# Second layer of a two-layer attention trunk: a pair's value products moved to stand ahead of the next pair's turn

## The chip, the core and the metric

The kernel runs on one core of a Trainium2 chip. The metric is the device time of one execution in microseconds, and less is better. A core has a matrix engine (TensorE, PE in the profile; its weight loads are PEld), a vector engine (VectorE, DVE), a scalar engine (ScalarE, ACT), a general one (GpSimd, POOL) and a queue that starts transfers (SyncE, SP). Each works through its own instructions in order and waits for the others on semaphores.

## The reference

Two decoder layers over 256 tokens of width 2048, in fp32. Each layer is x + (mixer(rmsnorm(x)) * silu(gate)) @ w_out; the first mixer is latent attention with 16 heads, the second, which the change touches, is sliding-window attention with 32 query heads of width 64, 4 key and value heads and a learned sink per head. A last RMSNorm ends it.

```python
def swa_sink_attention(q, k, v, sinks):          # blocks of 128 queries against 256 keys
    s = jnp.einsum('bnqhgd,bnkhd->bnhgqk', qb, kw) * (D ** -0.5)
    s = jnp.where(valid, s, NEG_INF)             # causal, window of 128
    m = jnp.maximum(jnp.max(s, axis=-1, keepdims=True), sink)
    e = jnp.exp(s - m)
    p = e / (jnp.sum(e, axis=-1, keepdims=True) + jnp.exp(sink - m))
    return jnp.einsum('bnhgqk,bnkhd->bnqhgd', p, vw)

x = x + (y * jax.nn.silu(gate)) @ w_out
```

## The kernel before

**Precision and products.** The activations lie transposed: channels on the partitions, the 256 tokens along the free axis. An fp32 product is made of three matmuls on values split into a high and a low half (`proj`, lines 247 to 252: high weights by high data, high weights by low data, low weights by high data). All weights (some 114 MB with the rest of what is read) stream in pieces of 128 x 1024. `Weights` (lines 49 to 96) loads a piece through SP's queue (L70), splits it (high half by ScalarE, L89; low half by VectorE, L90) and hands the pieces out in the order in which they were added. It keeps four pairs of halves. A *slab* (line 254) is one piece's work: 8 chunks of the contraction by 3 matmuls, 24 matmuls of 128 x 256. Two slabs make one output chunk of 128 channels; their sums lie in one of three PSUM banks (tag `pp`).

**The second layer's attention.** It goes through 16 pairs of heads, c = 0 to 15. For a pair there are:

- `query(c)` (line 616): two slabs, then rotary embedding on VectorE (lines 293 to 296) and a split into a stack of high and low halves (`stack_pair`, lines 302 and 303). It is a generator that stops behind its first slab and again at its end.
- `gate(c)` (line 627): two slabs, and silu (lines 361 to 363), likewise a generator with a stop behind each slab.
- `scores(c)` (line 635): six matmuls (L642, L644, L645), then softmax: masked minimum on VectorE (L322, L324), exponentials on ScalarE (L328), the sum with the sink, a reciprocal, and the normalised probabilities (L333, L334).
- `turn(p)` (line 336): six transposes of the probabilities on TensorE (L342, L343), and their split into `pth` (ScalarE, L348) and `ptl` (VectorE, L349), one buffer each.
- `values(c)` (line 660): six matmuls of values by probabilities (L670, L672) into the one bank `yp`, two copies (ScalarE, L675) and two adds (VectorE, L679), which leave `y`.
- `gated(c)` (line 682): `y` times the gate (L684), and its split into the two halves `ys[c]` (ScalarE L194, VectorE L195), which the output projection reads.

The loop (line 692) works ahead: in turn c it does the query of pair c + 2 and the scores of pair c + 1. In program order a turn is: query slab, turn c, scores c + 1, query slab, gate slab, values c, gate slab, gating c. In the last two turns there is no query; gate slabs stand in its place, and the values follow on the second gate slab.

**The output projection.** 14 chunks (line 712) of two slabs each over `ys[0]` to `ys[15]`; the last pair's `ys[15]` is the last contraction chunk of the second slab. The last two chunks (lines 721 to 774) are done apart, with the final norm.

**What sets the order.** The program's order is a wish: at compile time a planner gives each engine its instructions, by program order, but moves later ones ahead where it expects an earlier one to wait. What was given to an engine it does in that order. In the second layer's attention TensorE's order is the program's, except at the start (pair 0) and at the end (pair 15), where transposes and values stand between the matmuls of a slab.

Of the kernel before, what the change touches and what calls it, by code (L numbers as in the profile page):

```python
# [28 lines left out]
KC = D // P  # L29
# [19 lines left out]
class Weights:  # L49
# [43 lines left out]
    def next(self):  # L93
        self.split(self.used + 1 + self.ahead_split)
        self.used += 1
        return self.ready.popleft()
# [3 lines left out]
def trunk(ctx: ExitStack, tc: tile.TileContext, a: dict):  # L100
# [49 lines left out]
    def xc(c):  # L150
        return x_t[c // XQ][:, c % XQ, :]
# [37 lines left out]
    def tiny(name, n=2, bufs=2):  # L189
        return work.tile([P, n], F32, tag=name, name=name, bufs=bufs)  # L190
# [56 lines left out]
    def proj(ps, lhs, rhs, first, last):  # L247

        wh, wl = lhs
        mm(ps, lhsT=wh, rhs=rhs[:, 0, :], start=first, stop=False)  # L250
        mm(ps, lhsT=wh, rhs=rhs[:, 1, :], start=False, stop=False)  # L251
        mm(ps, lhsT=wl, rhs=rhs[:, 0, :], start=False, stop=last)  # L252

    def slab(ps, half, src):

        hi, lo = w.next()
        k0 = half * (KC // 2)
        for k in range(k0, k0 + KC // 2):
            n = slice((k - k0) * P, (k - k0 + 1) * P)
            proj(ps[:, 0:S], (hi[:, n], lo[:, n]), src[k], k == 0, k == KC - 1)  # L260

    def bank(pool_, tag):
        return pool_.tile([P, 512], F32, tag=tag, name=tag)
# [26 lines left out]
    def rope(out, ps, cs, sn, mask):  # L290
        t1 = work.tile([P, S], F32, tag="ro1", name="ro1")
        t2 = work.tile([P, S], F32, tag="ro2", name="ro2")
        dve.tensor_tensor(out=t1, in0=ps, in1=cs, op=ALU.mult)
        dve.stream_shuffle(out=t2, in_=ps, mask=mask)
        dve.tensor_tensor(out=t2, in0=t2, in1=sn, op=ALU.mult)
        dve.tensor_tensor(out=out, in0=t1, in1=t2, op=ALU.add)  # L296

    def stack_pair(dst, src):

        for j, r in ((0, slice(0, 64)), (1, slice(64, 128))):  # L300
            o = slice(64, 128) if j == 0 else slice(0, 64)
            act.copy(out=dst[r, j, :], in_=src[r, :])  # L302
            dve.tensor_tensor(out=dst[o, j, :], in0=src[r, :], in1=dst[r, j, :].bitcast(F32), op=ALU.subtract)  # L303
# [9 lines left out]
    def softmax(ps, j, nm, sm, mask, scale, sink):  # L313

        p = work.tile([P, 3 * P], F32, tag="p", name="p", bufs=3)
        for i in range(2):
            cols = slice(0, P) if i == 0 else slice(P, 3 * P)
            src = ps[:, 0:P] if i == 0 else ps[:, S:2 * S]
            m = mask
            if i == 0:  # L320
                m = p[:, cols]
                dve.tensor_tensor(out=m, in0=ps[:, P:S], in1=mask[:, P:], op=ALU.add)  # L322
            c = 2 * i + j
            dve.tensor_tensor_reduce(out=p[:, cols], in0=src, in1=m,  # L324
                                     scale=scale if isinstance(scale, float) else scale[:, i:i + 1],
                                     scalar=BIG if sink is None else sink, op0=ALU.add, op1=ALU.min,
                                     accum_out=nm[:, c:c + 1])
            act.activation(out=p[:, cols], in_=p[:, cols], func=AF.Exp, scale=-1.0, bias=nm[:, c:c + 1],  # L328
                           accum_out=sm[:, c:c + 1])
        return p  # L330
# [25 lines left out]
    def silu(ps, rB):  # L356

        hx = work.tile([P, S], F32, tag="hx", name="hx", bufs=2)
        th = work.tile([P, S], F32, tag="th", name="th", bufs=1)
        out = work.tile([P, S], F32, tag="sg", name="sg", bufs=2)  # L360
        dve.scalar_tensor_tensor(out=hx, in0=ps, scalar=0.5, in1=rB, op0=ALU.mult, op1=ALU.mult)
        act.activation(out=th, in_=hx, func=AF.Tanh)
        dve.scalar_tensor_tensor(out=out, in0=th, scalar=1.0, in1=hx, op0=ALU.add, op1=ALU.mult)
        return out
# [251 lines left out]
    def query(c):  # L616
        ps = bank(ps_p, "pp")
        slab(ps, 0, hs)
        yield
        slab(ps, 1, hs)  # L620
        qf = work.tile([P, S], F32, tag="ro3", name="ro3")
        rope(qf, ps[:, 0:S], cos1R, sin1R, MASK_SWA)
        qs_of[c] = work.tile([P, 2, S], F32R, tag="qs", name="qs", bufs=2)
        stack_pair(qs_of[c], qf)
        yield

    def gate(c):
        ps = bank(ps_p, "pp")
        slab(ps, 0, hs)
        yield  # L630
        slab(ps, 1, hs)
        sg_of[c] = silu(ps[:, 0:S], r1B)
        yield

    def scores(c):
        kv = 2 * c // (QH // KVH)
        nm, sm, ri = tiny("nm", 4), tiny("sm", 4), tiny("ri", 4)
        pair = []
        for j in range(2):
            sc = bank(ps_s, "sc")  # L640
            o, t = sc[:, 0:S].rearrange("p (a q) -> p a q", a=2), slice(0, P)
            mm(o, lhsT=qs_of[c][:, j, t], rhs=k1s[kv][:, :, t], start=True, stop=True)  # L642
            o, t = sc[:, S:2 * S], slice(P, S)
            mm(o, lhsT=qs_of[c][:, j, t], rhs=k1s[kv][:, 0, :], start=True, stop=False)  # L644
            mm(o, lhsT=qs_of[c][:, j, t], rhs=k1s[kv][:, 1, :], start=False, stop=True)  # L645
            h = 2 * c + j
            pair.append(softmax(sc, j, nm, sm, mask_w, -SWA_SCALE, nsink[:, h:h + 1]))

        e = tiny("es", 4)
        dve.tensor_tensor(out=e.rearrange("p (i j) -> p i j", j=2), in0=nm.rearrange("p (i j) -> p i j", j=2),  # L650
                          in1=sinks[:, 2 * c:2 * c + 2].rearrange("p (i j) -> p i j", i=1).to_broadcast([P, 2, 2]),
                          op=ALU.add)
        act.activation(out=e, in_=e, func=AF.Exp)
        dve.tensor_tensor(out=e, in0=e, in1=sm, op=ALU.add)
        dve.reciprocal(out=ri, in_=e)
        for j in range(2):
            normalise(pair[j], ri, j)
        p_of[c] = pair

    def values(c):  # L660

        kv = 2 * c // (QH // KVH)
        v0, v1 = (v[:, kv, :, :].rearrange("p a d -> p (a d)") for v in vs)
        pt = pt_of.pop(c)
        yp = bank(ps_y, "yp")
        late = yp.rearrange("p (j i q) -> p j i q", j=2, i=2)[:, :, 1, :]
        for n, p in enumerate(pt):
            for j in range(2):
                o = slice(j * S, (j + 1) * S)
                mm(yp[:, o], lhsT=v0, rhs=p[:, o], start=n == 0 and j == 0, stop=False)  # L670
        for n, p in enumerate(pt):
            mm(late, lhsT=v1, rhs=p[:, 4 * P:].rearrange("p (j q) -> p j q", j=2), start=False, stop=n == 1)  # L672
        t = work.tile([P, S], F32, tag="vh", name="fo", bufs=1)
        for j in range(2):
            act.copy(out=t[j * HD:(j + 1) * HD, :], in_=yp[(1 - j) * HD:(2 - j) * HD, j * S:(j + 1) * S])  # L675
        y = work.tile([P, S], F32, tag=("vl", "v1")[c % 2], name="y", bufs=1)
        for j in range(2):
            n = slice(j * HD, (j + 1) * HD)
            dve.tensor_tensor(out=y[n, :], in0=yp[n, j * S:(j + 1) * S], in1=t[n, :], op=ALU.add)  # L679
        y_of[c] = y  # L680

    def gated(c):
        yg = work.tile([P, S], F32, tag="yg", name="yg", bufs=2)
        dve.tensor_tensor(out=yg, in0=y_of.pop(c), in1=sg_of.pop(c), op=ALU.mult)  # L684
        split(ys[c], yg)

    for c in range(2):
        for _ in query(c):
            pass
        if c == 0:  # L690
            scores(0)
    for c in range(KC):
        q, gt = query(c + 2) if c + 2 < KC else iter([None, None]), gate(c)
        next(q)
        if c + 2 >= KC:
            next(gt)
        pt_of[c] = turn(p_of.pop(c), True)
        if c + 1 < KC:
            scores(c + 1)
        next(q)  # L700
        if c + 2 < KC:
            next(gt)
        if c + 2 < KC:
            values(c)
        next(gt)
        if c + 2 >= KC:
            values(c)
        gated(c)


    sq_x2 = Squares("sq_x2")
    for c in range(KC - 2):
        ps = bank(ps_p, "pp")
        for half in range(2):
            slab(ps, half, ys)
        dve.tensor_tensor(out=xc(c), in0=ps[:, 0:S], in1=xc(c), op=ALU.add)
        sq_x2.add(xc(c))
        dve.tensor_scalar(out=xc(c), in0=xc(c), scalar1=gf[:, c:c + 1], scalar2=None, op0=ALU.mult)
# [137 lines left out]
```

## Time and profile before

| what | value |
|---|---|
| median of 3 runs | 684.73 us (680.62 to 688.16) |
| profiled execution | 684.75 us, its span 683.0 us |
| mean granted TensorE clock | 0.996 |
| layer 1, projection in (0 to 60 us) | TensorE busy 55.79 of 60.00 us |
| layer 1, attention (60 to 257) | 195.96 of 197.00 |
| layer 1, projection out (257 to 353.5) | 96.50 of 96.50 |
| layer 2, keys, values, first queries (353.5 to 390) | 36.27 of 36.50 |
| layer 2, the 16 pairs (390 to 590) | 199.54 of 200.00 |
| layer 2, projection out, norm, end (590 to 683) | 83.22 of 93.00 |

How to read the profile: times in us from the start of the span; a row of stages gives the stretch, its length, and for each engine the busy time and the count of instructions, then TensorE's granted clock, the share of the transfer engines and GB/s. A count holds the instructions that were begun before the stretch and still run in it; a matmul stands for some 0.28 us in the trace, though the next one starts after less than half of that, so two or so are counted too many. A row of instructions gives start, length, engine, line, operation, output <- inputs, and in brackets how long the engine idled before it and for whom. A row of a group gives count, busy time, mean length in ns, and the idle time ahead of the group.

### The profile page before, as it was taken

What the parts mean: (1) busy time and instruction counts of PE and PEld (TensorE: products, weight loads), DVE (VectorE), ACT (ScalarE), POOL (GpSimd) and SP (SyncE); (2) the same over time, 40 slices, a digit from 0 to 9 for tenths busy, and PEclk for the clock granted to TensorE, in tenths of its full rate; (3) what the DMA queues carried; (4) which work ended last, traced back from release to release, by engine and by line L of the source; (5) the groups of instructions that cost most, each with busy time, mean ns of one, the idle gap of its engine ahead of it and who ended that gap; (6) DMA issues with size and microseconds to landing.
All of it is one profiled execution on the core that took longest, in us unless ns stands there. A gap on an engine that the chain in (4) does not pass through costs nothing.

```text
span 683.0 us, 14550 instructions
## 1 busy us (share of the span) xinstructions
PE 667.3 (98%) x5718; PEld 663.1 (97%) x5718; DVE 532.2 (78%) x1085; ACT 428.0 (63%) x853; POOL 66.3 (10%) x72
## 2 busy tenths in 40 slices
PE   8999999999999999999999999999999999999994
PEld 7999999999999999999999999999999999999994
DVE  5897787787688686666658899998998998766664
ACT  6667656666676665444446688788778778544430
POOL 3634000000000000111110000000000000022220
PEclk9999999999999999999999999999999999999998
DMA  8664454554554555555554545545445454455604
GB/s 311 252 206 168 161 161 144 185 167 144 183 162 150 174 167 174 196 183 189 184 187 160 180 141 169 166 147 177 160 157 158 157 177 158 156 188 195 204 32 124
DMA packets 37302, 117.00 MB, mean 171 GB/s; under 512 B 4209, under 2 KB 8945, under 8 KB 37233
## 3 DMA queue, kind: packets, MB, share of 16 engines
q1 hardware_dynamic: 37232, 116.06, 51.3%
q8 instruction: 45, 0.74, 0.4%
q14 instruction: 25, 0.20, 0.1%
HBM read 113.95 MB, written 2.10 MB: 170 GB/s over the span
## 4 chain that ended last, share of the span: by engine, by line
PE 88%; DVE 4%; ACT 3%; POOL 1%; issue 1%; DMA 1%; SPq 0%; DVEq 0%; ACTq 0%; POOLq 0%
PE pp L251 24%; PE pp L250 24%; PE pp L252 24%; PE pt L342 1%; DVE wlo L90 1%; ACT whi L89 1%; PE pp L735 1%; PE pp L520 1%; PE pp L522 1%; PE pp L521 1%; PE yp L670 1%; PE pt L343 1%; DVE x L762 1%; DMA wraw<-in_w_c 1%; PE sc L642 1%
## 5 line engine op out<-in xcount | busy, mean ns | idle before, releaser
L90 DVE TENSOR_TENSOR wlo<-wraw,whi 128x1024 fp32r<-128x1024 f32 (+1 forms) x217 | 259.9, 1199 | 88.6 <-ACT whi L89 87.0
L89 ACT CAST whi<-wraw 128x1024 fp32r<-128x1024 f32 (+1 forms) x217 | 222.9, 1029 | 168.7 <-PE pp L251 142.1
L252 PE MATMUL pp<-hs,wlo 128*128 128x256 f32 x860 | 239.6, 279 | 1.3 <-DVE wlo L90 1.2
L250 PE MATMUL pp<-hs,whi 128*128 128x256 f32 x860 | 240.4, 280 | 0.4 <-ACT whi L89 0.4
L251 PE MATMUL pp<-hs,whi 128*128 128x256 f32 x860 | 239.6, 279 | 0.5 <-DVE hs L200 0.5
L252 PEld LDWEIGHTS pp<-hs,wlo 128*128 128x128 f32 x860 | 161.5, 188 | 1.9 <-DVE wlo L90 1.9
L250 PEld LDWEIGHTS pp<-hs,whi 128*128 128x128 f32 x860 | 162.6, 189 | 0.6 <-ACT whi L89 0.6
L251 PEld LDWEIGHTS pp<-hs,whi 128*128 128x128 f32 x860 | 161.6, 188 | 0.9 <-DVE hs L200 0.9
L251 PE MATMUL pp<-ys,whi 128*128 128x256 f32 x480 | 133.9, 279 | 0.1
L250 PE MATMUL pp<-ys,whi 128*128 128x256 f32 x480 | 133.9, 279 | 0.0
L252 PE MATMUL pp<-ys,wlo 128*128 128x256 f32 x480 | 133.8, 279 | 0.0
L216 POOL TENSOR_TENSOR sq_x<-sq_x,sq 128x256 f32<-128x256 f32 x43 | 53.3, 1240 | 577.2 <-ACT sq L215 335.5
L250 PEld LDWEIGHTS pp<-ys,whi 128*128 128x128 f32 x480 | 91.2, 190 | 0.0
L251 PEld LDWEIGHTS pp<-ys,whi 128*128 128x128 f32 x480 | 90.1, 188 | 0.3 <-DVE ys L195 0.3
L252 PEld LDWEIGHTS pp<-ys,wlo 128*128 128x128 f32 x480 | 90.1, 188 | 0.0
L328 ACT ACTIVATE p<-p,nm 128x128 f32<-128x128 f32 x96 | 42.7, 446 | 15.3 <-DVE nm L324 15.3
L250 PE MATMUL pp<-cq,whi 128*128 128x256 f32 x96 | 27.3, 284 | 0.0
L200 DVE SCALAR_TENSOR_TENSOR hs<-x,gains,hs 128x256 fp32r<-128x256 f32 x32 | 24.9, 790 | 2.6 <-ACT hs L199 2.6
L252 PE MATMUL pp<-cq,wlo 128*128 128x256 f32 x96 | 26.7, 278 | 0.0
L251 PE MATMUL pp<-cq,whi 128*128 128x256 f32 x96 | 26.7, 278 | 0.0
L303 DVE TENSOR_TENSOR qs<-ro,qs 64x256 fp32r<-64x256 f32 x48 | 20.2, 421 | 7.5 <-ACT qs L302 6.3
L302 ACT CAST qs<-ro 64x256 fp32r<-64x256 f32 x48 | 19.2, 400 | 8.3 <-DVE ro L296 7.7
(242 smaller groups left out, 1133.6 us busy)
## 6 DMA issues: line engine op xcount, KB each, us to landing
wraw<-in_w_g SPq DMA_DIRECT2D x64, 512.0 KB, 3.7
wraw<-in_w_o SPq DMA_DIRECT2D x64, 512.0 KB, 3.5
wraw<-in_w_q SPq DMA_DIRECT2D x32, 512.0 KB, 3.6
wraw<-in_w_ukv SPq DMA_DIRECT2D x16, 512.0 KB, 3.5
wraw<-in_w_c SPq DMA_DIRECT2D x15, 512.0 KB, 6.7
wraw<-in_w_uq SPq DMA_DIRECT2D x8, 512.0 KB, 3.6
wraw<-in_w_uq SPq DMA_DIRECT2D x8, 256.0 KB, 2.6
wraw<-in_w_k SPq DMA_DIRECT2D x4, 512.0 KB, 3.4
```

Source lines behind the costliest of these rows:

```text
L89: self.nc.scalar.copy(out=hi, in_=src)
L90: self.nc.vector.tensor_tensor(out=lo, in0=src, in1=hi.bitcast(F32), op=ALU.subtract)
L200: dve.scalar_tensor_tensor(out=dst[:, 1, :], in0=src, scalar=col, in1=dst[:, 0, :].bitcast(F32), op0=ALU.mult, op1=ALU.subtract)
L216: pool.tensor_tensor(out=self.acc, in0=self.acc, in1=t, op=ALU.add)
L250: mm(ps, lhsT=wh, rhs=rhs[:, 0, :], start=first, stop=False)
L251: mm(ps, lhsT=wh, rhs=rhs[:, 1, :], start=False, stop=False)
L252: mm(ps, lhsT=wl, rhs=rhs[:, 0, :], start=False, stop=last)
L302: act.copy(out=dst[r, j, :], in_=src[r, :])
L303: dve.tensor_tensor(out=dst[o, j, :], in0=src[r, :], in1=dst[r, j, :].bitcast(F32), op=ALU.subtract)
L328: act.activation(out=p[:, cols], in_=p[:, cols], func=AF.Exp, scale=-1.0, bias=nm[:, c:c + 1], accum_out=sm[:, c:c + 1])
L342: nc.tensor.transpose(t[:, 0, j * S + i * P:j * S + (i + 1) * P], p[:, i * P:(i + 1) * P], ident)
L343: nc.tensor.transpose(t[:, 1, j * P:(j + 1) * P], p[:, 2 * P:3 * P], ident)
```

## The change

In the loop over the pairs, the generators of the gates are made ahead, so that both slabs of a gate stand next to each other. The value products and the gating of pair c - 1 stand in turn c, behind the first query slab and directly ahead of the transposes. In turn 14 the first slab of gate 14 takes the place of the query slab; behind the scores stand its second slab and both slabs of gate 15. In turn 15 only values 14, gating 14 and the transposes are left. Values 15 and gating 15 stand between the two slabs of the first output chunk. The order in which the weights are used is the same, and so is every instruction.

```diff
-    for c in range(KC):
-        q, gt = query(c + 2) if c + 2 < KC else iter([None, None]), gate(c)
-        next(q)
-        if c + 2 >= KC:
-            next(gt)
+    ends = [gate(c) for c in range(KC)]
+    for c in range(KC):
+        if c + 2 < KC:
+            q = query(c + 2)
+            next(q)
+        elif c + 1 < KC:
+            next(ends[c])
+        if c > 0:
+            values(c - 1)
+            gated(c - 1)
         pt_of[c] = turn(p_of.pop(c), True)
         if c + 1 < KC:
             scores(c + 1)
-        next(q)
         if c + 2 < KC:
-            next(gt)
-        if c + 2 < KC:
-            values(c)
-        next(gt)
-        if c + 2 >= KC:
-            values(c)
-        gated(c)
+            next(q)
+            next(ends[c])
+            next(ends[c])
+        elif c + 1 < KC:
+            next(ends[c])
+            next(ends[c + 1])
+            next(ends[c + 1])
...
     for c in range(KC - 2):
         ps = bank(ps_p, "pp")
         for half in range(2):
             slab(ps, half, ys)
+            if c == 0 and half == 0:
+                values(KC - 1)
+                gated(KC - 1)
```

## The prediction

> **What bounds the kernel now.** I read the page first, then a table of stages, then the waits of the second layer's attention, and last the start times of single matmuls. The page says that TensorE is the bound; the column 1.00 of the stages below, that its clock is granted in full.
>
> ```profile
> span 683.0 us, 14550 instructions
> PE 667.3 (98%) x5718; PEld 663.1 (97%) x5718; DVE 532.2 (78%) x1085; ACT 428.0 (63%) x853; POOL 66.3 (10%) x72
> ```
>
> The profiled execution took 684.75 us, its span 683.0 and 1.75 around it; the median of the runs shown is 684.73, so a sum against the one stands against the other. The three runs lie 7.5 us apart, so within 1% (6.85 us) is about what a measurement can't tell from no change.
>
> The stages, with busy time (and count) of TensorE, its weight loads, VectorE, ScalarE and GpSimd:
>
> ```profile
> 400.09:570.77 170.68, 170.68 (x1484) 170.68 (x1483) 157.89 (x404) 133.51 (x312) 0.00 (x0) 1.00 0.49 163
> 401.43:406.87 5.44, 5.44 (x50) 5.44 (x49) 5.41 (x19) 3.42 (x11) 0.00 (x0) 1.00 0.56 197
> 407.56:413.21 5.65, 5.65 (x50) 5.65 (x49) 4.84 (x12) 4.93 (x11) 0.00 (x0) 1.00 0.52 186
> 558.99:564.43 5.44, 5.44 (x50) 5.44 (x49) 5.44 (x18) 3.47 (x10) 0.00 (x0) 1.00 0.57 188
> 565.12:570.77 5.65, 5.65 (x50) 5.65 (x49) 4.79 (x10) 4.83 (x11) 0.00 (x0) 1.00 0.53 186
> 570.77:589.28 18.51, 18.05 (x152) 17.42 (x151) 15.66 (x36) 12.99 (x29) 0.00 (x0) 1.00 0.44 143
> 100.63:106.09 5.46, 5.46 (x51) 5.46 (x49) 3.87 (x15) 4.10 (x14) 0.00 (x0) 1.00 0.60 197
> 106.86:112.20 5.34, 5.34 (x49) 5.34 (x48) 3.80 (x5) 2.58 (x5) 0.00 (x0) 1.00 0.45 164
> 260.00:350.00 90.00, 90.00 (x767) 90.00 (x765) 58.97 (x65) 45.12 (x64) 15.36 (x15) 1.00 0.56 186
> 595.00:655.00 60.00, 60.00 (x532) 60.00 (x531) 40.00 (x45) 26.86 (x34) 16.03 (x11) 1.00 0.56 185
> ```
>
> The first row covers 13 pairs, from turn 1 to turn 14: 13.13 us each, TensorE without a gap, VectorE 92% busy. So in the steady part there is no stall that a new order could remove.
>
> But the next four rows show something else. Each holds two slabs, 48 matmuls of one shape (the count has some 2 more, begun before the window). Between the scores and the values they take 5.44 us, 113.3 ns each; between the values and the next turn 5.65 us, 117.7 ns each. The difference, 0.21 us, stands in the first pair shown as in the last. It does not belong to a slab, an engine's load or the clock (1.00 in all): the first layer's output projection holds the slow spacing over 90 us (90.00 / 765 = 117.6 ns), the second layer's the fast one over 60 us (60.00 / 530 = 113.2). It is a rhythm that TensorE keeps until something between two slabs tips it.
>
> The start times show where it tips:
>
> ```profile
> 406.76 0.28 PE L252 MATMUL pp<-hs,wlo 128*128 128x256 f32 x1
> 406.87 0.39 PE L670 MATMUL yp<-pth,vs 128*128 128x256 f32 x2
> ...
> 407.44 0.28 PE L672 MATMUL yp<-ptl,vs 128*128 128x256 f32 x1
> 407.56 0.28 PE L250 MATMUL pp<-hs,whi 128*128 128x256 f32 x1
> 413.21 0.38 PE L342 MATMUL pt<-ident,p 128*128 128x128 f32 x2
> ...
> 413.76 0.27 PE L343 MATMUL pt<-ident,p 128*128 128x128 f32 x1
> 413.79 0.37 PE L642 MATMUL sc<-k1s,qs 128*128 128x256 f32 x1
> ```
>
> The values (L670, L672) take 0.69 us at the fast spacing; the slab behind them runs slow. The transposes (L342, L343) and scores follow on the slow stretch; the slabs behind those run fast. The first layer has the other entry: its 48 matmuls ahead of a turn run fast (row 100.63) and so do those behind it (row 106.86), with no scores between. So a turn is left fast from either side.
>
> **The change part by part.** No instruction is added or removed, and the weights are used in the same order (for pair 14 and 15 too), so SP's queue of loads stays as it is. Three things move.
>
> *Pairs 0 to 13.* The values of pair c leave the middle of gate c, and stand behind the first query slab of the next turn, directly ahead of the transposes. Now the values still end fast, but transposes and scores come right behind, and then four slabs in a row. By the rows above these are all fast. There are 14 slow stretches now, behind the values of pairs 0 to 13: 14 x (5.65 - 5.44) = 2.94 us saved; the slab behind the values of pair 14 is slow too (24 x 4.4 ns = 0.1). The sum takes 3.05. From both sides: 0 if the turn needs a slow entry to be left fast, and the fast stretches lost as well if the tip carries through the turn (14 x -0.21 = -2.94).
>
> *What else the values move.* On VectorE and ScalarE the two copies, two adds, the gating and its split now come just ahead of the probabilities' split and the softmax. What TensorE next needs from there, and when:
>
> ```profile
> 566.56 0.49 ACT L334 ACTIVATE p<-p,ri 128x256 f32<-128x256 f32 x1
> 567.38 0.87 DVE L303 TENSOR_TENSOR qs<-ro,qs 64x256 fp32r<-64x256 f32 x2 [0.46 <-ACT qs L302]
> 570.77 0.38 PE L342 MATMUL pt<-ident,p 128*128 128x128 f32 x2
> 571.35 0.37 PE L642 MATMUL sc<-k1s,qs 128*128 128x256 f32 x1
> ```
>
> The normalised probabilities are ready at 567.05, 3.7 us ahead of their turn; the query stack at 568.25, 3.1 us ahead of its scores. The moved work ahead of them is at most
>
> ```profile
> L90 DVE TENSOR_TENSOR wlo<-wraw,whi 128x1024 fp32r<-128x1024 f32 x53 | 64.6, 1219 | 1.5 <-ACT whi L89 0.2
> L349 DVE TENSOR_TENSOR ptl<-pt,pth 128x768 fp32r<-128x768 f32 x13 | 12.4, 950 | 0.0
> L679 DVE TENSOR_TENSOR y<-yp,fo 64x256 f32<-64x256 f32 x26 | 11.0, 422 | 4.4 <-ACT fo L675 4.2
> L684 DVE TENSOR_TENSOR yg<-y,sg 128x256 f32<-128x256 f32 x13 | 5.5, 425 | 0.4
> L675 ACT COPY fo<-yp 64x256 f32<-64x256 f32 x26 | 9.5, 366 | 0.5
> L348 ACT CAST pth<-pt 128x768 fp32r<-128x768 f32 x13 | 10.3, 795 | 0.0
> L303 DVE TENSOR_TENSOR qs<-ro,qs 64x256 fp32r<-64x256 f32 x26 | 10.9, 421 | 6.2 <-ACT qs L302 5.8
> ```
>
> two adds (0.84 us) and, if nothing fills it, the wait for two copies (0.73); the gating stood ahead of the softmax before as well. 1.6 us fits into 3.1. I cost it at nothing; without that cover it is up to 1.6 us a pair once the slack is used up. The probabilities' split (0.80 and 0.95 us) had two slabs to finish in and now has four slabs and more, but there was no stall to save there except in the last pair.
>
> *The end, pairs 14 and 15 and the first output chunk.* Here TensorE does wait:
>
> ```profile
> 578.48 0.28 PE L251 MATMUL pp<-hs,whi 128*128 128x256 f32 x1
> 578.91 0.33 PE L342 MATMUL pt<-ident,p 128*128 128x128 f32 x1 [0.15 <-ACT p L333]
> 580.16 0.27 PE L343 MATMUL pt<-ident,p 128*128 128x128 f32 x1
> 580.19 0.36 PE L251 MATMUL pp<-hs,whi 128*128 128x256 f32 x1
> 583.75 0.28 PE L252 MATMUL pp<-ys,wlo 128*128 128x256 f32 x1
> 584.20 0.50 PE L670 MATMUL yp<-ptl,vs 128*128 128x256 f32 x2 [0.17 <-DVE ptl L349]
> 588.53 0.28 PE L250 MATMUL pp<-ys,whi 128*128 128x256 f32 x1
> 588.94 0.38 PE L251 MATMUL pp<-ys,whi 128*128 128x256 f32 x1
> ```
>
> From turn 14 (570.77) to the end of the first output chunk it takes 18.51 us. The same work without waits: five slabs of 24 matmuls at 113.3 ns (13.60), twice the values (1.38), turn 14 with its scores (401.43 - 400.09 = 1.34), and turn 15 (about 0.85, the 0.58 from 413.21 to 413.79 and the late start behind it): 17.2. So 1.3 us are lost now: at turn 15, which waits for its probabilities, at the values, which wait for the low half, and at the last pair's output, whose low half is late by 0.3. The change puts gate 15's second slab ahead of turn 15, so that about 8.9 us of products stand between scores 15 and turn 15 where they need 567.05 - 559.0 = 8.1 in pair 13 (the window from 558.99 begins as scores 14 end). That wait goes. But values 15 then have only half a chunk (2.7 us) behind their turn, and the output chunk needs pair 15 after 45 matmuls and the values, 45 x 0.1133 + 0.69 = 5.8 us after the turn. The chain there, 0.80 + 0.95 for the split, 0.69 values, two copies 0.73, two adds 0.84, gating 0.43 and two halves of its split at about 0.42, makes 5.3 if nothing stands in it, and weight splits (1.22 each) and the work of another pair do stand in it; in this trace it took from 580.16 to 588.94, 8.8: up to 3.0 late. The planner fills such waits: the transposes of pair 15 stand inside a slab already (an L251 of it follows them at 580.19), and products of the output chunk stand ahead of the low half of the values (583.75). I take 1.0 lost there: 1.0 - 1.3 = -0.3, with bounds of -1.3 and +1.7.
>
> **The sum.** 684.75 - 3.05 - 0.3 = 681.4 us, provided that the output projection stays in the fast rhythm.
>
> The Trainium skill ("TensorE: Matmul & The Clock Gate", section LDWEIGHTS) puts a load of weights at its columns / 1.2 ns, an estimate of 107 ns for 128, near the 113 ns that a matmul and its load take here. It knows one spacing for a shape (section Back-to-back issue gap); the two spacings in the rows above differ from that, and by the Trainium skill alone the first term would be zero.
>
> **The rivals.**
> 1. *The output projection tips to slow.* Values 15 now stand inside the first chunk with no turn behind them, and values entered fast have been left slow in every pair. From there the 648 matmuls left of chunks 0 to 13 and the 96 of the last two, at 4.4 ns more, cost 3.3 us: 684.7. For it: the first layer's projection, which also follows its last value products, is slow throughout (row 260). Against: the values of pair 15 were entered after a wait in this trace, and row 595 is fast; waits for values 15 or for their output are likely to come again.
> 2. *One spacing a pair, whatever the order.* If the rhythm goes by how much lies between two slabs, each pair keeps half slow and half fast, and only the end is left: 684.4. The Trainium skill's single spacing, named above, gives this too. Against it: four stretches of 48 that repeat to 0.01 us.
> 3. *Slow throughout* (the other side). The tip by the values carries through transposes and scores when nothing lies between. Then all four slabs run slow: +2.94 for the 14 fast stretches, and +3.3 if the projection stays slow behind them: 684.75 + 2.94 + 3.3 - 0.3 = 690.7, or 687.4 with a fast projection. It decides from the first pair on, with 0.21 us each. For it: no place in this trace has values directly ahead of a turn, so nothing shows what the turn does then. Against it: row 106.86, a turn entered and left fast.
> 4. *VectorE becomes the bound.* It has 157.89 / 13 = 12.15 us of work a pair and idles 0.98; a fast pair of 12.92 leaves 0.77. The waits now are for the copies (4.4 us in 13 pairs) and the query's casts (6.2). If the chain from values to gating leaves another 1.6 us open, a pair needs 12.15 + 0.98 + 1.6 = 14.7; but four weight splits a pair (1.22 each) can stand in such holes, so I count half: 13.9, 0.8 over now, 14 x 0.8 = 11 less the slack of 3.1 and with no gain: about 692. It decides once holes exceed 0.98 a pair.
>
> **How the numbers follow.** Forecast (fast pairs, fast projection) 0.42; rival 1 0.25; rival 2 0.13; rival 3 0.13; rival 4 0.07. The first three lie between 680 and 687 with the end's bounds; rival 3 reaches to 690.7. With the runs' own spread I give 678.5 to 689.0, which leaves out most of rival 4, the upper end of rival 3 and the lowest runs; the forecast's own range is 680.4 to 683.4. Faster by over 1% (under 677.9) would need gains beyond every term here: 0.04. Slower by over 1% (over 691.6) is rival 4 and the top of rival 3: 0.06. The rest, 0.90, is within 1%.
>
> **What would show it.** Right: a pair from turn to turn takes 12.92 us in place of 13.13; all four slabs of a pair start every 113.3 ns; turn 15 starts without a wait; TensorE has no idle time between turn 1 and turn 14. Rival 1 shows as 117.7 ns from the second half of the first output chunk on. Wrong: 117.7 ns behind the scores (rival 3), unchanged 13.13 (rival 2), or TensorE waiting for the query stack, the probabilities or weight halves in the steady part (rival 4).

## The result, and the profile after

The changed kernel takes 681.24 us in the median of 19 runs (677.14 to 687.57) against 684.71 (680.62 to 688.33) in 19 runs of the kernel before on the same chip: ratio 0.9942, 95% interval 0.9928 to 0.9957. The forecast was 681.4.

The execution that was profiled took 677.14 us, 4.1 under the median. Its page, the span and the busy time of the engines:

```profile
span 675.3 us, 14552 instructions
PE 659.8 (98%) x5718; PEld 655.7 (97%) x5718; DVE 530.4 (79%) x1085; ACT 428.6 (63%) x853; POOL 66.3 (10%) x72
```

The span is 7.7 us shorter, twice what the median lost, so not all of it can be the change. The stages of the changed kernel, with the columns of before (window, length, TensorE, weight loads, VectorE, ScalarE, GpSimd):

```profile
396.18:564.14 167.96, 167.96 (x1485) 167.96 (x1483) 155.90 (x405) 134.06 (x313) 0.00 (x0) 1.00 0.51 165
397.53:408.41 10.88, 10.88 (x98) 10.88 (x97) 9.98 (x29) 8.14 (x21) 0.00 (x0) 1.00 0.49 156
552.57:563.45 10.88, 10.88 (x98) 10.88 (x97) 9.96 (x30) 8.45 (x21) 0.00 (x0) 1.00 0.56 177
564.14:581.74 17.60, 17.52 (x155) 17.33 (x154) 15.96 (x37) 12.78 (x31) 0.00 (x0) 1.00 0.49 157
260.00:350.00 90.00, 90.00 (x797) 90.00 (x796) 61.25 (x67) 46.37 (x66) 15.88 (x15) 1.00 0.60 193
590.00:650.00 60.00, 60.00 (x532) 60.00 (x531) 40.00 (x45) 26.82 (x34) 16.24 (x12) 1.00 0.56 177
```

From turn 1 to turn 14 the same 13 pairs take 167.96 us in place of 170.68: 12.92 a pair, 0.21 less. Rows two and three are the first pair and the last of them: the four slabs of a pair, now in one stretch, take 10.88 us, 96 matmuls at 113.3 ns. From turn 14 to the end of the first output chunk it takes 17.60 us in place of 18.51. That is 2.72 + 0.91 = 3.6 of the 7.7 us. Most of the rest stands ahead of turn 1, which starts at 396.18 in place of 400.09. Of these 3.9 us 0.21 is the change too: pair 0 loses its slow stretch (from the first slab behind the scores of turn 0 to turn 1, 391.14 to 400.09 before and 387.44 to 396.18 after, 8.95 and 8.74 us). That makes 3.84 us for the change. The other 3.7 came from code that it does not touch, and row five shows why: the first layer's output projection ran at 90.00 / 795 = 113.2 ns here (117.6 in the profile of before), and it has 816 matmuls: 816 x 4.5 ns = 3.7 us.

So each of the two long output projections runs in one of two spacings (the prediction calls them rhythms), and much of a run's time follows from how many of them were slow. The profiles hold three such cases of the changed kernel and of before: changed, both fast, 677.14 (above); before, the first one slow, 684.75; changed again, both slow, 684.39 (run r_after below). Adding or taking 3.7 us for the first projection and 3.3 (744 matmuls) for the second puts before with both fast at 681.0 and with both slow at 688.1, where its fastest and slowest runs lie (680.62 and 688.33; that these are the two cases is argued from the sum, no profile fell on them). Not every run fits: four of before at 686.4 to 687.6 and one of the changed kernel at 687.57 lie at none of these levels, and what they lose is not known. Like against like, the change is worth 677.14 - 681.0 = -3.9 or 684.39 - 688.1 = -3.7 us, on both sides of the 3.84 that the stages give.

Where the values meet the turn, single matmuls of the changed kernel (start, duration, line, operands):

```profile
408.30 0.28 PE L252 MATMUL pp<-hs,wlo 128*128 128x256 f32 x1
408.41 0.39 PE L670 MATMUL yp<-pth,vs 128*128 128x256 f32 x2
...
408.98 0.28 PE L672 MATMUL yp<-ptl,vs 128*128 128x256 f32 x1
409.10 0.38 PE L342 MATMUL pt<-ident,p 128*128 128x128 f32 x2
...
409.67 0.37 PE L642 MATMUL sc<-k1s,qs 128*128 128x256 f32 x1
...
410.45 0.28 PE L250 MATMUL pp<-hs,whi 128*128 128x256 f32 x1
```

The values still take 0.69 us (408.41 to 409.10), and the transposes follow without a gap.

### The profile page after: what moved, and what is told of

The parts are those of the page before. It is cut to its first block, busy times and chain, and to the rows that moved or that the text cites. A ratio compares the mean times of both kernels' runs of the same rounds, so it can differ in the third digit from the quotient of the medians.

```text
span 675.3 us, 14552 instructions
## 1 busy us (share of the span) xinstructions
PE 659.8 (98%) x5718; PEld 655.7 (97%) x5718; DVE 530.4 (79%) x1085; ACT 428.6 (63%) x853; POOL 66.3 (10%) x72
## 4 chain that ended last, share of the span: by engine, by line
PE 89%; DVE 4%; ACT 3%; POOL 1%; issue 1%; DMA 1%; SPq 0%; DVEq 0%; ACTq 0%; POOLq 0%
PE pp L251 24%; PE pp L250 24%; PE pp L252 24%; ACT whi L89 2%; PE pt L342 2%; DVE wlo L90 1%; PE pp L744 1%; PE pp L520 1%; PE pp L522 1%; PE pp L521 1%; PE yp L670 1%; DMA wraw<-in_w_c 1%; PE pt L343 1%; DVE x L771 1%; PE sc L642 1%
## 5 line engine op out<-in xcount | busy, mean ns | idle before, releaser
L250 PE MATMUL pp<-ys,whi 128*128 128x256 f32 x480 | 132.6, 277 | 0.0
L251 PE MATMUL pp<-ys,whi 128*128 128x256 f32 x480 | 132.5, 276 | 0.0
L252 PE MATMUL pp<-ys,wlo 128*128 128x256 f32 x480 | 132.3, 276 | 0.0
L194 ACT CAST ys<-yg 128x256 fp32r<-128x256 f32 x32 | 12.2, 404 | 29.4 <-DVE yg L684 27.8
```

What stands on the lines that cost most here:

```text
L194: act.copy(out=dst[:, 0, :], in_=src)
```

## The experiments

The theory of the prediction: a short odd group between slabs sets the spacing of the slabs behind it; the value products, entered fast, leave it slow, a turn with scores leaves it fast. Its rivals: the saving comes from somewhere else (values that come later and so spread VectorE's work; the end; chance in the projections), or the slow stretch is a property of one operation, such as the strided output of the late value products (L672).

Because a whole run can move by 3 to 4 us with an untouched projection, most verdicts below rest on the length of a pair in the profile, which repeats to 0.01 us, and the run times stand beside it. A run of an edit is written with the kernel it starts from. Every ratio is against the kernel before on the chip of that run, and its median differs from chip to chip: 684.71 us with the result above and 684.76 with runs 5 to 7, but 681.32 with runs 1 to 4, 681.44 with 8 to 10 and 681.29 with 11. On the latter most runs of before lie under 683 us (25 of 35 with runs 1 to 4), on the former two one in 19 and one in 11. So the run times of an edit show little unless they are compared level by level.

**1. The pairs alone** (from the changed kernel; turns 14 and 15 and the output chunk as before).

```diff
-        if c > 0:
+        if 0 < c < KC - 1:
             values(c - 1)
             gated(c - 1)
...
-            next(ends[c + 1])
-            next(ends[c + 1])
+            values(c)
+            gated(c)
...
-            if c == 0 and half == 0:
-                values(KC - 1)
-                gated(KC - 1)
```

> Pairs 0 to 13 in the changed order, pairs 14 and 15 and the first output chunk as before. Rhythm theory: a pair from turn to turn takes 12.92 us in the profile, the end from turn 14 on keeps its waits; the gain is 14 x 0.21 = 2.9 us of the whole, about 681.8 us. Rival 'the end does it': pairs give nothing that counts, about 684.7. Rival 'the probabilities' split was late' (the values gain by coming a turn later, not by their neighbours): 12.92 us as well.

Measured: 680.88 us (12 runs, 677.88 to 685.45), ratio 0.9983 (0.9946 to 1.0019). Of its profiled run, the slabs ahead of turn 1's values and the slabs behind turn 1 and its scores; then the stages:

```profile
391.50:399.51 8.01, 8.01 (x71) 8.01 (x69) 7.20 (x22) 6.97 (x19) 0.00 (x0) 1.00 0.44 140
401.00:411.70 10.70, 10.70 (x97) 10.70 (x96) 10.20 (x29) 8.22 (x22) 0.00 (x0) 1.00 0.46 151
400.22:568.18 167.96, 167.96 (x1484) 167.96 (x1483) 155.95 (x404) 134.37 (x313) 0.00 (x0) 1.00 0.50 164
568.18:586.69 18.51, 18.06 (x152) 17.43 (x151) 16.30 (x38) 13.28 (x31) 0.00 (x0) 1.00 0.44 143
590.00:650.00 60.00, 60.00 (x512) 60.00 (x511) 37.95 (x42) 25.93 (x32) 14.63 (x10) 1.00 0.57 187
```

The pairs take 12.92 us and the end 18.51, to the hundredth the one length of after and the other of before: the two parts are independent. The first two rows show more: here the slabs ahead of the values ran slow (some 68 matmuls in 8.01 us, 118 ns), and those behind the scores fast all the same (some 95 in 10.70, 113). So the joined group of values, turn and scores was left fast from a slow entry as well. The last row shows the second output projection at 60.00 / 510 = 117.6 ns: the price of the first rival, though with the end of before. The first projection was slow in this run too, which took 685.45 us, 2.6 under the 688.1 of before with both slow; the fastest six runs take 677.9 to 678.9.

**2. The end alone** (from the changed kernel; pairs 0 to 13 as before).

```diff
-        if c > 0:
+        if c + 1 == KC:
             values(c - 1)
             gated(c - 1)
...
             next(ends[c])
+            values(c)
             next(ends[c])
+            gated(c)
```

> Pairs 0 to 13 as before, pairs 14 and 15 and the first output chunk in the changed order. Rhythm theory: a pair keeps 13.13 us; only the waits of the end go, 0.9 to 1.1 us between turn 14 and the first output chunk, about 683.7 us. Rival 'the end does it': the whole gain, about 681.

Measured: 682.1 us (12 runs, 679.23 to 684.72), ratio 0.9993 (0.9962 to 1.0024).

```profile
400.44:571.12 170.68, 170.68 (x1484) 170.68 (x1483) 157.84 (x404) 133.55 (x312) 0.00 (x0) 1.00 0.50 163
571.12:588.73 17.61, 17.53 (x154) 17.34 (x153) 15.42 (x35) 12.57 (x29) 0.00 (x0) 1.00 0.49 155
```

Pairs as before, the end 0.9 shorter. The fastest runs of each, if they are those with both projections fast, add up as well: 681.0 before (worked out above; its lowest runs on this chip lie at 680 to 681.5), 677.9 to 678.9 with the pairs alone, 679.2 to 680.6 with the end alone.

**3 and 4. The dose: one slab, or three, between values and turn.** In run 3 (from the changed kernel) the values stand ahead of the query slab (one slab behind them before the turn), in run 4 (from the kernel before) ahead of both gate slabs and behind the second query slab (the first query slab of the next turn follows, so three); run 4 has the end of before. Before has two, the changed kernel none.

```diff
     for c in range(KC):
+        if c > 0:
+            values(c - 1)
+            gated(c - 1)
         if c + 2 < KC:
             q = query(c + 2)
             next(q)
         elif c + 1 < KC:
             next(ends[c])
-        if c > 0:
-            values(c - 1)
-            gated(c - 1)
```

The first cut is run 3's edit of the changed kernel. Run 4 edits the kernel before, and the middle of its turn then reads:

```python
        if c + 2 < KC:
            next(q)
            values(c)
            next(ends[c])
            next(ends[c])
```

> As the changed kernel, but the values stand ahead of the query slab, so that one slab of 24 matmuls lies between the values and the turn. Rhythm theory: that slab runs at 117.8 ns, the other three at 113.3; a pair takes 12.92 + 24 x 4.4 ns = 13.03 us, half of the gain of the pairs is lost, about 682.7 us. Rival 'the values gain by coming a turn later': the values still come a turn later, so 12.92 us and 681.2 us. Rival 'rhythm by how much lies between two slabs': a break more in the pair, 13.13.

> As the kernel before, but the values stand a slab earlier, behind the second query slab, so that three slabs lie between the values and the next turn. Rhythm theory: three slabs at 117.8 ns, one at 113.3; a pair takes 13.13 + 24 x 4.4 ns = 13.23 us, 14 x 0.107 = 1.5 us more than before, about 686.2 us. Rivals by lateness of the probabilities' split: no change (its two halves end some 3.6 us behind the turn's start and the values would start 4.1 us behind it), or waits of TensorE ahead of the values and more than 13.23 us.

Measured: run 3 680.29 us (10 runs, 678.03 to 685.67), ratio 0.9975 (0.9939 to 1.0011); run 4 684.36 (10 runs, 682.41 to 686.92), ratio 1.002 (0.9989 to 1.0051). Run 3 in the profile, its last 12 pairs; then the slab ahead of turn 1 (400.15); then that pair and the next, each as the three slabs behind the scores and the slab behind the values:

```profile
413.44:569.72 156.28, 156.28 (x1371) 156.28 (x1369) 146.27 (x375) 122.11 (x288) 0.00 (x0) 1.00 0.50 163
397.30:400.10 2.80, 2.80 (x26) 2.80 (x25) 1.98 (x4) 2.71 (x7) 0.00 (x0) 1.00 0.79 250
401.60:410.00 8.40, 8.40 (x74) 8.40 (x72) 8.34 (x25) 5.89 (x17) 0.00 (x0) 1.00 0.39 126
410.80:413.40 2.60, 2.60 (x25) 2.60 (x24) 1.94 (x4) 2.42 (x5) 0.00 (x0) 1.00 0.70 221
414.80:422.90 8.10, 8.10 (x74) 8.10 (x73) 8.07 (x24) 6.16 (x17) 0.00 (x0) 1.00 0.45 145
423.70:426.40 2.70, 2.70 (x25) 2.70 (x25) 2.46 (x5) 2.32 (x5) 0.00 (x0) 1.00 0.71 215
```

and run 4, its 13 pairs:

```profile
399.77:571.85 172.08, 172.08 (x1484) 172.08 (x1483) 159.03 (x404) 132.75 (x312) 0.00 (x0) 1.00 0.49 161
```

156.28 / 12 = 13.02 and 172.08 / 13 = 13.24. With 0, 1, 2 and 3 slabs between values and turn a pair takes 12.92, 13.02, 13.13 and 13.24 us: a straight line of 0.107 us a slab, 24 x 4.45 ns. Where the values stand within the pair, and so when VectorE's work comes, shows no effect of its own here; the length goes by how many slabs lie between them and the next turn. But the first pair of run 3 went the other way: its turn was entered slow (some 24 matmuls in 2.80 us, 117 ns), the three slabs behind the scores ran slow too (some 71 in 8.40 us, 118 ns), the values were entered slow, and the slab behind them ran fast (about 23 in 2.60, 113). So a turn with scores does not always leave TensorE fast, and values entered slow left it fast.

**5. The strided products in the middle** (from the kernel before): the four products of L670 and the two of L672 trade places, so that a product with a plain output ends the group.

```diff
         for n, p in enumerate(pt):
+            if n == 1:
+                for m, r in enumerate(pt):
+                    mm(late, lhsT=v1, rhs=r[:, 4 * P:].rearrange("p (j q) -> p j q", j=2), start=False, stop=False)
...
-        for n, p in enumerate(pt):
-            mm(late, lhsT=v1, rhs=p[:, 4 * P:].rearrange("p (j q) -> p j q", j=2), start=False, stop=n == 1)
```

> As the kernel before, but of the six value products the two that write a strided output (L672) stand in the middle and not last; the last is a plain one of 128 x 256, as in a slab. If the strided product is what tips the rhythm, the two slabs behind the values run at 113.3 ns and a pair takes 12.92 us without any move, about 2.9 us less than before. If any change of the stream from slab to values and back tips it, 117.8 ns and 13.13 us stay.

Measured: 685.64 us in one run; from turn 1 to turn 14

```profile
400.97:571.66 170.69, 170.69 (x1485) 170.69 (x1484) 157.88 (x404) 133.49 (x312) 0.00 (x0) 1.00 0.49 163
```

as before, 13.13 a pair. The strided output as last of the group is not the cause.

**6. Six transposes behind the values** (from the kernel before), into a spare tile that nothing reads: they take the turn's place without its scores.

```diff
+    def tip(n):
+        t = ps_t.tile([P, 2, 512], F32, tag="pt", name="pt")
+        for i in range(n):
+            nc.tensor.transpose(t[:, i // 4, i % 4 * P:(i % 4 + 1) * P], ident, ident)
...
             values(c)
+            tip(6)
```

> As the kernel before, with six more transposes (of a constant, their result unused) behind the values of pairs 0 to 13, where the values stay in the middle of the gate. If transposes leave the fast rhythm whatever stands ahead of them, the two slabs behind them run at 113.3 ns (5.44 us) and a pair takes 13.13 + 0.85 - 0.21 = 13.8 us; if it takes the scores too, or another place, they stay at 117.8 (5.65 us) and a pair takes 14.0 us.

Measured: 691.74 us in one run; the 13 pairs

```profile
401.05:577.67 176.62, 176.62 (x1562) 176.62 (x1561) 157.96 (x405) 132.87 (x312) 0.00 (x0) 1.00 0.48 157
409.30:414.60 5.30, 5.30 (x49) 5.30 (x48) 4.43 (x8) 4.07 (x10) 0.00 (x0) 1.00 0.56 197
```

are 13.59 each. The two slabs behind the transposes ran at 113 ns in every pair (the second row is one of them, some 47 matmuls in 5.30 us), so 13.13 - 0.21 + t = 13.59 and t = 0.67 us for six transposes. Behind the values they bring the fast spacing back, at three times the price of the slow stretch. The turns of this run were entered fast from a slab, and were left fast.

**7. The same six transposes ahead of the first layer's output projection** (from the changed kernel, one `tip(6)` behind that layer's last value products), and the changed kernel again on the same chip.

> As the changed kernel, with six more transposes (of a constant, their result unused) behind the last value products of the first layer, ahead of its output projection. Rhythm theory: that projection's 816 matmuls then run at 113.3 ns in every run; runs that had it slow gain 3.7 us less 0.85, about 678 us, and the spread of the runs shrinks; runs that had it fast lose 0.85. If its rhythm in a run comes from something else (the chip, the loads), 117.8 ns stays in some runs and the time rises by 0.85 us in all.

> The changed kernel once more, beside the others on one chip. Rhythm theory: two heaps of run times, some 3.7 us apart (816 x 4.5 ns), by the rhythm of the first layer's projection, which the change doesn't touch; and a pair of 12.92 us in any run.

Measured: run 7 677.94 us (6 runs: four at 677.7 to 678.0, two at 682), ratio 0.9902 (0.987 to 0.9934) against 684.76 before; the changed kernel 681.16 (7 runs: six at 680.6 to 681.9, one at 684.39), ratio 0.9927 (0.99 to 0.9954). The run of the changed kernel that was profiled, the 13 pairs and the two projections:

```profile
400.30:568.27 167.97, 167.97 (x1485) 167.97 (x1483) 155.90 (x405) 134.07 (x313) 0.00 (x0) 1.00 0.50 165
260.00:350.00 90.00, 90.00 (x767) 90.00 (x766) 59.12 (x65) 45.33 (x65) 15.07 (x15) 1.00 0.57 186
590.00:650.00 60.00, 60.00 (x511) 60.00 (x511) 38.51 (x43) 25.61 (x32) 14.99 (x11) 1.00 0.59 192
```

Here both projections are slow (some 765 in 90 us, 509 in 60), and the time is the 684.39. In run 7's profile, one of its two runs at 682, the first projection is slow in spite of the transposes:

```profile
260.00:350.00 90.00, 90.00 (x766) 90.00 (x765) 58.35 (x65) 44.76 (x65) 14.81 (x14) 1.00 0.57 184
```

So the transposes there helped in four runs of six at most: 677.8 would be a fast first projection with their 0.67 us added, but no run at that time has a profile. By its median it is the fastest version measured, and not a reliable one.

**8. The transposes inside both projections** (from the changed kernel, behind their second chunk).

```diff
+        if c == 1:
+            tip(6)
```

> As the changed kernel, with six transposes of a constant (result unused) behind the second output chunk of both output projections, where the stream has run in slabs for some 5 us and no wait is left. If a turn tips the rhythm to fast from either side, both projections run at 113.3 ns behind it in every run; each six cost 0.67 us, so some 678.5 us in one heap, where the changed kernel lies at 681 with a slow first projection and 684 with both slow. If six transposes keep the rhythm that they find (as in the profile of the kernel that had them right behind the first layer's last value products), the heaps stay and lie 1.3 us later, about 682.5.

Measured: 684.9 us (12 runs, 682.65 to 685.63), ratio 1.0031 (1.0009 to 1.0053). The first projection ahead of the transposes, behind them, and the second behind its own:

```profile
256.63:266.00 9.37, 9.37 (x85) 9.37 (x84) 6.25 (x11) 4.87 (x8) 0.00 (x0) 1.00 0.46 153
270.00:350.00 80.00, 80.00 (x681) 80.00 (x681) 52.78 (x57) 39.50 (x56) 15.05 (x15) 1.00 0.55 185
592.00:652.00 60.00, 60.00 (x512) 60.00 (x511) 38.17 (x43) 25.37 (x32) 15.98 (x11) 1.00 0.56 182
```

Some two of a count began before the window: 9.37 / 83 = 113 ns ahead of the transposes, 80.00 / 679 = 117.8 behind, and 60.00 / 510 = 117.6 in the second. In run 6 values and six transposes together, entered fast, were left fast; here the six alone, entered fast, were left slow. The median of 684.9 misses both expected times, 678.5 and 682.5.

**9 and 10. The same edit in the first layer, alone and with the transposes of run 8.** In run 9 the first layer's values stand directly ahead of its turn as well, with second buffers for what then lives longer (from the changed kernel; run 10 has both).

```diff
-        if mixes:
-            mixes()
...
+                if mixes:
+                    mixes()
...
-        kf = work.tile([P, 2, S], F32, tag="f2", name="kf", bufs=1)
+        kf = work.tile([P, 2, S], F32, tag="qs", name="kf")
```

> As the changed kernel, and in the first layer too the value products of a group (of two heads) stand directly ahead of the next group's turn (two buffers in place of one for their operands, three for the gates, one for two scratch tiles to make room). Rhythm theory: the 60 matmuls or so that run at 117.8 ns behind the value products there run at 113.3; a group takes 24.40 - 0.27 = 24.13 us, 7 groups 1.9 us, about 679.3 us beside 681.2. Rival: another thing than the values tips the rhythm there (the scores do, or the products for the values), then 24.40 us stay and the time is that of the changed kernel.

> Both additions together. Rhythm theory: 678.5 - 1.9 = 676.6 us, the fastest of all, in one heap. If six transposes keep the rhythm that they find, 680.6 and heaps; if the first layer's move gives nothing, that of the kernel with the transposes alone.

Measured: run 9 685.34 us (12 runs, 681.93 to 686.45), ratio 1.0029 (1.0008 to 1.005); run 10 686.59 (12 runs, 683.76 to 689.64), ratio 1.0053 (1.0027 to 1.0079). In run 9 a group of the first layer from turn to turn, in it the slabs behind the turn and those behind the scores, and the wait of TensorE in that layer:

```profile
106.18:131.22 25.04, 24.70 (x215) 24.49 (x214) 19.00 (x40) 16.15 (x32) 0.00 (x0) 1.00 0.48 158
106.88:116.37 9.49, 9.49 (x87) 9.49 (x85) 7.36 (x15) 5.55 (x9) 0.00 (x0) 1.00 0.40 122
124.77:130.00 5.23, 5.23 (x47) 5.23 (x46) 3.18 (x13) 4.23 (x14) 0.00 (x0) 1.00 0.45 141
```

```profile
PE sc L543 <- DVE kk L509: 2.2, 6, 0.5
```

The same group in the changed kernel, with another start:

```profile
106.33:130.73 24.40, 24.40 (x215) 24.40 (x213) 18.91 (x40) 15.78 (x32) 0.00 (x0) 1.00 0.48 162
```

0.64 us more a group, 4.5 in seven. TensorE now waits for the rotated keys, which come out of VectorE behind the moved work, and a slow stretch is still there: the slabs behind the turn run fast (9.49 / 84), those behind the scores slow (5.23 / 44.5). This failed twice over: here the moved work had no cover, and the weight loads are idle for 25.04 - 24.49 = 0.55 us of the group, where they have no gap in the changed kernel. Run 10, expected at 676.6, missed it by 10 us. Its first projection, ahead of its transposes and behind them, then the second one in the same way:

```profile
260.50:270.00 9.50, 9.50 (x83) 9.50 (x83) 6.21 (x10) 4.75 (x8) 0.00 (x0) 1.00 0.41 122
275.00:350.00 75.00, 75.00 (x664) 75.00 (x663) 50.75 (x56) 39.13 (x55) 13.76 (x13) 1.00 0.59 193
588.00:591.70 3.70, 3.70 (x35) 3.70 (x34) 2.88 (x4) 2.04 (x3) 0.00 (x0) 1.00 0.21 65
592.50:652.50 60.00, 60.00 (x512) 60.00 (x511) 38.20 (x42) 25.63 (x33) 15.97 (x11) 1.00 0.57 185
```

In the first, 117.3 ns ahead (81 matmuls) and 113.3 behind (662): slow into fast, the opposite of run 8 with the same six instructions. In the second, some 33 matmuls in 3.70 us (113) ahead and 60.00 / 510 = 117.6 behind: fast into slow again. Run 8's second was entered fast too (587.20 to 590.60, some 30 matmuls in 3.40 us). So at all four places of runs 8 and 10 six transposes alone in a stream of slabs swapped the spacing; that they always do is not shown.

**11. Transposes and six score-like products inside the first projection** (from the changed kernel, behind its second chunk), the nearest copy of the turn that leaves the slabs fast.

```diff
+        if c == 1:
+            tip(6)
+            like_scores()
```

> As the changed kernel, with six transposes and six matmuls in the forms of the scores (on data at hand, results unused) behind the second output chunk of the first layer's projection. So far transposes alone have turned a slow stream fast and a fast one slow, while transposes and scores were followed by a fast stream from either side. If the two together set the rhythm, the 720 matmuls behind them run at 113.3 ns in every run, for 1.34 us more: one heap at 678.5 us (another at 681.8 where the second layer's projection falls slow), where the changed kernel has its heaps at 677 and 681. If they too only shift it, the first projection is slow in some runs and the upper heap lies at 682.5.

Measured: 688.53 us (12 runs: two at 679.2, two at 682, eight at 688.1 to 689.6), ratio 1.0071 (1.0038 to 1.0103). The profiled run is one of the two at 679.2:

```profile
257.50:267.50 10.00, 10.00 (x87) 10.00 (x86) 6.59 (x11) 4.81 (x8) 0.00 (x0) 1.00 0.46 161
272.00:350.00 78.00, 78.00 (x691) 78.00 (x690) 52.57 (x57) 40.50 (x57) 14.85 (x14) 1.00 0.57 190
```

Entered slow (85 in 10.00 us), left fast (689 in 78.00, 113.2 ns). The eight runs at 688 to 690 are 9 to 10 us above it, more than the 6.5 that two slow projections behind the break would add; none of them has a profile, and what they lose stays open.

## Why the prediction was right, step by step

1. *Four slabs at 113.3 ns in the pairs.* Right in size and in the place of the loss: 12.92 us a pair in all 13, 2.72 measured where 13 of the 14 slow stretches (2.73) lie, and 0.21 in pair 0. The line of runs 1 to 4 shows that it is the slabs behind the values that pay, not the place of the values. With that the rival of one spacing whatever the order falls (it gave 13.13 a pair), and the one of slow throughout (13.34). The Trainium skill ("TensorE: Matmul & The Clock Gate", section Back-to-back issue gap) gives one sustained spacing for each width that it lists, by which this term was zero; here the measurement decides.
2. *The reason given was too broad.* "So a turn is left fast from either side" holds for the 13 pairs of before (entered slow) and of run 6 (entered fast), and for the joined group of the changed kernel, entered fast in its 13 pairs and slow once in run 1. It does not hold as a rule: in the first pair of run 3 a turn entered slow was left slow, in run 8 six transposes turned fast into slow and in run 10 slow into fast. A short odd group can swap the rhythm as well as set it; entries of nearly the same form went different ways. The row 106.86 on which the step leaned was one case of several, a turn without scores. That the order chosen is one that repeats could not be known from it: in this the prediction had luck.
3. *VectorE's moved work at nothing.* Right. Its work is 155.90 / 13 = 12.0 us of 12.92 a pair, and TensorE's busy time fills the whole window. The fourth rival falls. Run 9 shows the price of moved work without cover, up to 0.64 us a group.
4. *The end, -0.3, was mis-sized: -0.91, inside its bounds.* The wait of turn 15 is gone, as said. 0.1 of the 0.91 is the slow slab behind the values of pair 14, which the prediction had counted in its first term and, as part of the 1.3 us lost, a second time here. What was too high was the 1.0 us for the late chain of pair 15. In the changed kernel:

```profile
577.73 0.39 PE L670 MATMUL yp<-pth,vs 128*128 128x256 f32 x2
578.20 0.51 PE L670 MATMUL yp<-ptl,vs 128*128 128x256 f32 x2
578.78 0.28 PE L250 MATMUL pp<-ys,whi 128*128 128x256 f32 x1
...
582.18 0.49 PE L250 MATMUL pp<-ys,whi 128*128 128x256 f32 x2
582.52 0.52 PE L251 MATMUL pp<-ys,whi 128*128 128x256 f32 x2
582.87 0.40 PE L252 MATMUL pp<-ys,wlo 128*128 128x256 f32 x2
```

   Two products that follow each other at 113 ns take 0.23 us; from 577.73 to 578.20 it is 0.47, so the low half of the probabilities is late by 0.24, and from 582.18 to 582.87, four products, by as much. The rest of the chain stands behind products of the next chunk, which the planner had put there. The column of weight loads shows the sum: idle 18.51 - 17.42 = 1.09 us in the stage before, 17.60 - 17.33 = 0.27 after.
5. *"Provided that the output projection stays in the fast rhythm."* It did in the profiled run, and in run r_after it did not:

```profile
582.91:586.33 3.42, 3.42 (x33) 3.41 (x31) 2.78 (x6) 1.53 (x5) 0.00 (x0) 1.00 0.35 92
587.23:660.00 72.77, 72.77 (x620) 72.77 (x619) 47.02 (x53) 32.08 (x40) 17.44 (x12) 1.00 0.49 160
```

   The first rival is real and costs what it was priced at, but with one and the same order it comes in some runs and not in others, and it did not begin where the prediction put it, behind the values. The 30 products behind values 15 still ran fast (30 starts in 3.42 us); the slow spacing (72.77 / 618 = 117.7) begins behind the short wait for pair 15's output, 586.33 to 587.23. In the profile of 677.14 the same wait was followed by the fast one. The prediction had taken the first projection, slow in the profile of before, as fixed; it varies as well, fast in one profile of the changed kernel and slow in the other, and the levels of the run times say the same of before.

   That the forecast lies 0.2 us from the median is therefore in part luck: on the chip of the result most runs of before and of the changed kernel lay at the level of one slow projection (684.7 and 681), so that the medians differ by about the change. On the chips of runs 1 to 4 and 11 the kernel before itself has a median of 681.3, the time that was forecast for the changed one. The forecast gain was 3.35 us, the medians differ by 3.5, and the terms come to 14 x 0.21 + 0.91 = 3.85; the part of the end that was sized too small, some 0.5, is what it lacked.

Not settled is what makes the two rhythms. The strided output is ruled out (run 5) and the clock is granted in full in both (1.00). Which entry leads to which could not be told in advance for a projection. That the slow slabs are what the pairs lost is shown; why a group of instructions sets or swaps the spacing is not.

## What to carry to other kernels

In a stage in which TensorE shows 100% busy, divide the stage by the count of equal matmuls: two stretches of one shape at different spacing mean that there may be time to gain though the profile has no wait. Try the short odd groups next to each other, so that fewer long streams are entered (here 0.21 us a pair gained; in the first layer, run 9, 0.64 us a group lost), and test it by the length of the repeating stage, not by the whole time. Where run times of one kernel fall into levels, find which untouched stage varies before reading a median, and compare like with like.

## What the runs showed of the hardware that was not expected

- One shape (128x128 weights, 256 columns) has two spacings at the full clock, 113.3 and 117.8 ns, and TensorE holds one for hundreds of matmuls (816 in the first projection, over 90 us), with 100% busy in both. Short groups between slabs can change it: six transposes did so in either direction (runs 8 and 10), six value products too (before; first pair of run 3), and in run r_after it changed behind a short wait.
- The same program takes the one or the other in the same stage from run to run; with 3.7 and 3.3 us for the two projections this gives, by the sum, levels near 681, 684.7 and 688 for the kernel before and 677, 681 and 684.4 for the changed one.
- Six transposes of 128x128 in a stream of slabs cost 0.67 us, by the length of run 6's pairs. In run 8 it is 0.57 from the first of them to the next slab's first product,

```profile
267.50 0.82 PE L339 MATMUL pt<-ident 128*128 128x128 f32 x6
268.07 0.37 PE L250 MATMUL pp<-ys,whi 128*128 128x256 f32 x1
268.27 0.28 PE L251 MATMUL pp<-ys,whi 128*128 128x256 f32 x1
```

  and that product takes 0.20 us to the next in place of 0.12.
